# Neighbourhood attention over 416 keys in one run: latents in blocks of eight columns, biases expanded in DRAM

## The chip, the cores and the metric

The kernel runs on one core of a Trainium2 chip. The metric is the device time of one execution in microseconds (us), as the median of several executions. TensorE (PE) multiplies matrices, VectorE (DVE) and ScalarE (ACT) work on vectors, GpSimd (POOL) does vector work and starts DMAs, SyncE (SP) only starts DMAs. 16 DMA engines serve the core.

## The reference

Two layers of a diffusion transformer over 256 latents (4 rows of 64 columns) and 256 context tokens, width 1024, all in float32. Layer 0 mixes by retention, layer 1 by neighbourhood attention (32 heads of 32), each followed by an MLP of width 4096. Scales, shifts and gates come from `ada_w`, a projection of the conditioning vector. The part that the change touches:

```
rows = n // GRID_W                      # 4
kh = min(NAT_WIN_ROWS, rows)            # 4: every row is seen
kw = NAT_WIN_COLS                       # 16
row_start = jnp.clip(jnp.arange(rows) - kh // 2, 0, rows - kh)
col_start = jnp.clip(cols - kw // 2, 0, GRID_W - kw)
col_in = (cols[None, :] >= col_start[:, None]) & (cols[None, :] < col_start[:, None] + kw)
...
bias = rpb_f[:, dr_idx[None, :, None], dc_idx[:, None, :]]
bias = jnp.where(col_in[:, None, :], bias, -jnp.inf)
s_loc = jnp.einsum('bqhd,bikhd->bhqik', q_r, k_band) + bias
s_ctx = jnp.einsum('bqhd,blhd->bhql', q_r, k_c)
prob = jax.nn.softmax(jnp.concatenate([s_loc, s_ctx]), axis=-1)
```

A query sees, in each of the four rows, the 16 columns around its own, and all 256 context tokens. Its bias depends on the head, on the row difference (7 values are used) and on the column difference.

## The kernel before

**Matrix products.** Each float32 operand is split into a high and a low part (`hi`, `lo`); a product is three matmuls (`mm3`: high by high, high by low, low by high). Weights come in blocks of 512 KB: SP starts the load (`raw`, a ring of four buffers that the `ada_w` blocks, `rawa`, share), ACT casts `raw` to `hi`, DVE subtracts to get `lo` (five buffers of each).

**Order.** SP's instructions keep the order of the program (`PIN = {"sync"}`); the other engines' instructions are ordered by a scheduler, except where the text switches the order on. Every instruction is recorded at line L84, so groups are told apart by their tiles. `bg()` advances a stream in the background: one load of `ada_w` (`rawa`, SP) and its weighted sum on DVE (`acc`).

**Layer 0's MLP** runs twice over halves of the hidden width (`hf`), eight blocks (`fp`) each, then the second product. In it the bias of layer 1 is prepared in DRAM: `outside()` writes the negated table to `rpb_neg` (ACT's DMA queue) and fills `rpb_rows` with 1e30 (`far`, 14 DMAs of SP); `shifted_biases(q)`, called in `hf` 0 for `fp` 2 to 5, writes for each of the 64 query columns the 16 columns that it sees at the place of their key (79 DMAs of POOL, two for a query whose columns lie in both halves, each of 224 pieces, 32 heads by 7 row differences). `rpb_rows` is laid out by query column, head, half (32 columns), row difference, column.

**Latent order in layer 1.** `mod_aff` and `mod_split` put the latents, which come row by row, into two halves of 32 columns (`b=2`), each with its four rows, 128 latents a half. A query tile (`qt`) is a half. The keys of a head are kept in `kT` as half 0, half 1, context (512 columns).

**Attention.** 16 steps `n`: group of four heads `g = n // 2`, query tile `n % 2`. `scores(n)` forms 128 queries by 512 keys for four heads, four matmuls side by side in row groups of 32, three times (high and low parts). `soften(n)` adds the negated bias and takes the minimum in one DVE instruction per head; ACT takes the exponential with the sum. The bias tile is double: `load_bias(n + 2)` stands in `gather(n)`, in four or eight DMAs of POOL; the tile holds the bias of the 256 latent keys, and a two-part access (`bias_ap`) reads 256 zeros for the context behind them. Of the other half only the eight nearest columns can be seen; `gather` copies their 32 exponentials together (POOL), `flip` turns own half, context and these with PE transposes, and `attend` multiplies by the values. For the eight columns of the other half `rest_mm` picks the values by a selection matrix that POOL copies together (`sel`).

`q_evac` and `k_evac` split the projections into high part (ACT) and low part (DVE). Between the steps PE works on the next projections (`K`, `Q`, `V`) and on the output projection (`W`), in an order that the program writes out. PSUM has eight banks of 512 columns, given out in turn to all products, so a new product may have to wait until an earlier one is evacuated.

Of the kernel before, what the change touches and what calls it, by code (L numbers as in the profile page):

```python
# [10 lines left out]
F32 = mybir.dt.float32  # L11
F32R = mybir.dt.float32r
AF = mybir.ActivationFunctionType
# [91 lines left out]
def kernel(  # L105
# [60 lines left out]
    def tsl(t):  # L166
        return slice(t * P, (t + 1) * P)
# [225 lines left out]
    rpb_neg = dram.tile([NH, 15, 31], F32, tag="rpbn", name="rpb_neg")  # L393

    def outside():
        neg = scr("neg")
        act.dma_start(out=neg[:NH, :465], in_=rpb_in.rearrange("h r c -> h (r c)"))
        pool.tensor_scalar_mul(out=neg[:NH, :465], in0=neg[:NH, :465], scalar1=-1.0)
        act.dma_start(out=rpb_neg[:].rearrange("h r c -> h (r c)"), in_=neg[:NH, :465])
        far = scr("far")  # L400
        pool.memset(far[:], BIG)
        dst = rpb_rows[:].rearrange("q (a h) b d c -> (q a) (h b d c)", a=2)
# [3 lines left out]
    def shifted_biases(q):  # L406
        cs = min(max(q - 8, 0), GRID_W - 16)
        for b in range(2):
            c0, c1 = max(cs, HALFW * b), min(cs + 16, HALFW * (b + 1))
            if c0 < c1:  # L410
                src = rpb_neg[:, 4 : 4 + NRR, 15 - q + c0 : 15 - q + c1]
                pool.dma_start(out=rpb_rows[q][:, b, :, c0 - HALFW * b : c1 - HALFW * b], in_=src)


    pool.memset(onecol[:], 0.0)
# [178 lines left out]
    def mod_aff(pt, half, t, A, B, on_act=None, halves=False):  # L594

        tmp = scr("aff")
        for i in range(4):
            k = 4 * half + i
            a, b = A[:, k, t // 2 : t // 2 + 1], B[:, k, t // 2 : t // 2 + 1]
            o, x_ = tmp[:, tsl(i)], pt[:, tsl(i)]  # L600
            if halves:
                o = o.rearrange("p (b r c) -> p b r c", b=2, r=2)
                x_ = x_.rearrange("p (r b c) -> p b r c", b=2, r=2)
            if not (half if on_act is None else on_act):
                dve.tensor_scalar(out=o, in0=x_, scalar1=a, scalar2=b, op0=ALU.mult, op1=ALU.add)
            else:
                act.activation(out=o, in_=x_, func=AF.Identity, scale=a, bias=b)
        return tmp

    def mod_split(tmp, half, t, eng, halves=False):  # L610
        ks = slice(4 * half, 4 * half + 4)
        if halves:
            hi, lo = (
                h[:, ks, :NLAT].rearrange("p k (b r) -> p k b r", b=2)[:, :, :, 64 * t : 64 * t + 64]
                for h in (hTh, hTl)
            )
            split(tmp[:].rearrange("p (k b r) -> p k b r", k=4, b=2), hi, lo, eng)
# [661 lines left out]
    for hf in range(2):  # L1279
# [46 lines left out]
        for fp in range(len(hid), 8):  # L1326
            ht = hslot(fp)
            pb = [bank("p1") for _ in range(2)]
            us = take(2)
            mm1(us, ALL, pb)  # L1330
            pe.on = False
            dve.on = hf == 0
            evac1(pb, ALL, ht)
            if hf == 0 and fp < 6:
                residual(fp - 2, xns[fp - 2], gb, dve)
            dve.on = False
            hid.append(ht)
            if hf:
                bg(2 + fp % 2)
            elif fp > 5:  # L1340
                bg()
            if hf == 0 and fp < 6:
                for q in range(16 * (fp - 2), 16 * (fp - 1)):
                    shifted_biases(q)
        if G2 is None:
            G2 = load_gate(0, 1)
        for half in range(2):
# [142 lines left out]

    def k_evac(pb, g, a=0, b=NT):
        kT = kTs[g // 2][:, g % 2]
        act.copy(out=kT[:, 0, a:b], in_=pb[:, a:b])
        dve.tensor_sub(out=kT[:, 1, a:b], in0=pb[:, a:b], in1=kT[:, 0, a:b].bitcast(F32))

    def k_part(g, a=0, b=NT):
        k_evac(k_mm(g, a, b), g, a, b)
# [20 lines left out]

    ring = [None, None]

    def bias_at(n, j):
        i = 4 * (n % 2) + j
        return (ring[1], 0, 256) if i == 7 else (ring[0], i * 256, 7 * 256)

    def load_bias(n):

        g, qt = n // 2, n % 2
        parts = [(0, 4)] if n % 2 == 0 else [(0, 3), (3, 1)]
        for j0, nj in parts:
            tile_, o, _ = bias_at(n, j0)  # L1530
            b = tile_[:, o : o + 256 * nj]
            for r in range(4):
                pool.dma_start(
                    out=b[32 * r : 32 * r + 32].rearrange("p (h b c) -> p h b c", h=nj, b=2),
                    in_=rpb_rows[
                        HALFW * qt : HALFW * qt + HALFW, 4 * g + j0 : 4 * g + j0 + nj, :, 3 - r : 7 - r, :
                    ].rearrange("q h b d c -> q h b (d c)"),
                )

    def bias_ap(n, j):  # L1540
        tile_, o, zo = bias_at(n, j)
        base = tile_[:, o : o + 256]
        return bass.AP(base.tensor, base.offset, [list(base.ap[0]), [zo - o, 2], [1, 256]])
# [15 lines left out]

    def soften(n):  # L1560

        mn = smp.tile([P, 4], F32, tag="mn", name=nm("mn"), bufs=3)
        sm = sums[n] = smp.tile([P, 4], F32, tag="sums", name=nm("sums"), bufs=3)
        for j in range(4):
            s = Es[n, j] = scr("s")
            dve.tensor_tensor_reduce(
                out=s[:].rearrange("p (a t) -> p a t", a=2),
                in0=pss[n][j][:].rearrange("p (a t) -> p a t", a=2),
                in1=bias_ap(n, j),
                scale=1.0,  # L1570
                scalar=3.0e38,
                op0=ALU.add,
                op1=ALU.min,
                accum_out=mn[:, j : j + 1],
            )
            act.activation(
                out=s[:], in_=s[:], func=AF.Exp, scale=-1.0, bias=mn[:, j : j + 1], accum_out=sm[:, j : j + 1]
            )


    av = [None]
# [17 lines left out]

    def gather(n):  # L1600

        o = 0 if n % 2 else P
        c0 = 24 if n % 2 else 0
        for j in range(4):
            pool.tensor_copy(
                out=pt_at(n, RAW)[:, 32 * j : 32 * j + 32].rearrange("p (r c) -> p r c", r=4),
                in_=Es[n, j][:, o : o + P].rearrange("p (r c) -> p r c", r=4)[:, :, c0 : c0 + 8],
            )
        if n + 2 < NS:
            load_bias(n + 2)  # L1610

    def flip(n, sums_too=True):
        for j in range(4):
            pp = bank("ppt")
            for i, kc in enumerate((n % 2, 2, 3)):
                pe.transpose(pp[:, tsl(i)], Es[n, j][:, tsl(kc)], ident)
            w = 3 * P
            if j == 3:
# [48 lines left out]
    def rest_mm(half):  # L1667

        pr = bank("pnv")
        sels = scr("sel")  # L1670
        for qt in range(2):
            sel = sels[:, 32 * qt : 32 * qt + 32]
            pool.tensor_copy(
                out=sel.rearrange("p (r c) -> p r c", r=4),
                in_=ident.rearrange("p (r c) -> p r c", r=4)[:, :, 24 * qt : 24 * qt + 8],
            )
# [78 lines left out]
    pool.memset(ring[0][:, 7 * 256 :], 0.0)  # L1755
    pool.memset(ring[1][:, 256:1024], 0.0)
    load_bias(0)
    load_bias(1)
    for g in range(2):
        fetch(1)  # L1760
        k_part(g, NLAT, NT)
# [462 lines left out]
```

## Time and profile before

| | us |
|---|---|
| median of 3 runs | 1172.63 (1172.37 to 1175.64) |
| the profiled execution | 1173.14, its span 1171.0 |
| layer 0's MLP, `hf` 0 from `fp` 2 on (writing of the biases) | about 458 to 540 |
| `hf` 1, blocks `fp` 0 to 7, and what is prefetched for it | about 590 to 700 |
| the attention steps | about 813 to 965 |

How the rows are read: a row of the timeline or of the chain begins with the start and the length in us, then the engine, the operation, its tiles (output, arrow, inputs) and how many are drawn together (x). A group has its busy time and the mean of one in ns behind the bar, then the idle time before it and what ended that. A queue's row has packets, megabytes and the share of the time of 16 DMA engines. "PEld" is PE loading weights, beside its matmuls. `pqk` are scores, `s` the exponentials, `mn` the minima, `ppt` the transposed exponentials in PSUM and `pt` in SBUF, `pn` the projections of q and k, `pnv` of v, `pnw` the output projection, `pav` the attention's output.

### The profile page before, as it was taken

How to read it: one execution, taken by the hardware profiler on the slowest of the kernel's cores; microseconds unless marked ns; L12 is line 12 of the kernel's file. 1: busy time of each engine (PE TensorE's matmuls, PEld its weight loads, DVE VectorE, ACT ScalarE, POOL GpSimd, SP SyncE). 2: the span in 40 equal slices, each digit the busy share in tenths (PEclk: the TensorE clock that was granted, in tenths of full speed). 3: DMA queues.
4: the chain of work that ended last, by engine and by line, in shares of the span. 5: the costliest groups of instructions: out<-in, count | busy, mean ns of one | idle time of the engine just before them, and what ended most of it. 6: DMA issues, size and time to landing. Idle time of an engine off the chain costs nothing.

```text
span 1171.0 us, 17545 instructions
## 1 busy us (share of the span) xinstructions
PE 1160.9 (99%) x6687; PEld 980.6 (84%) x6687; DVE 850.3 (73%) x1363; ACT 480.8 (41%) x819; POOL 232.5 (20%) x418
## 2 busy tenths in 40 slices
PE   9999999999999999999999999999999999999997
PEld 7788888888888889888888888889888878999886
DVE  3787687777798877677866675578577589877457
ACT  3643332222323246442122333237466666756341
POOL 0102001010220241781211001223343430000001
PEclk9999999999999999999999999999999999999999
DMA  9943562544365426767666665637344335666761
GB/s 279 277 134 100 162 192 94 158 149 145 108 180 170 140 65 213 195 135 223 190 201 189 205 204 189 202 101 205 82 140 138 108 114 158 214 205 205 239 199 54
DMA packets 140115, 195.10 MB, mean 167 GB/s; under 512 B 9936, under 2 KB 81136, under 8 KB 140032
## 3 DMA queue, kind: packets, MB, share of 16 engines
q1 hardware_dynamic: 131904, 182.03, 50.6%
q0 software_dynamic: 6976, 9.39, 4.0%
q10 hardware_dynamic: 1152, 2.56, 0.7%
q8 instruction: 52, 0.85, 0.3%
q14 instruction: 31, 0.25, 0.1%
HBM read 189.12 MB, written 5.75 MB: 166 GB/s over the span
## 4 chain that ended last, share of the span: by engine, by line
PE 94%; DVE 2%; DMA 1%; ACT 1%; issue 1%; POOL 0%; ACTq 0%; DVEq 0%; SPq 0%
PE p L84 44%; PE pq L84 8%; PE pv L84 8%; PE pw L84 7%; PE pg L84 7%; PE pn L84 5%; PE pnv L84 4%; PE po L84 2%; PE ppt L84 2%; PE pnw L84 1%; PE pS L84 1%; PE pav L84 1%; PE pqk L84 1%; PE pt L84 1%; PE pada L84 1%; PE p1t L84 1%
## 5 line engine op out<-in xcount | busy, mean ns | idle before, releaser
L84 ACT CAST hi<-raw 128x1024 fp32r<-128x1024 f32 (+2 forms) x228 | 231.7, 1032 | 306.1 <-PE p L84 111.0
L84 DVE TENSOR_TENSOR lo<-raw,hi 128x1024 fp32r<-128x1024 f32 (+2 forms) x228 | 272.2, 1210 | 87.5 <-ACT hi L84 87.2
L84 PE MATMUL p<-hi,hid 128*128 128x512 f32 (+1 forms) x780 | 238.0, 386 | 0.0
L84 PEld LDWEIGHTS p<-hi,hid 128*128 128x128 f32 x780 | 145.8, 188 | 29.5
L84 PE MATMUL p<-hTl,hi 128*128 128x256 f32 (+1 forms) x512 | 165.9, 326 | 0.0
L84 PE MATMUL p<-hTh,lo 128*128 128x256 f32 (+1 forms) x512 | 165.9, 326 | 0.0
L84 PE MATMUL p<-hTh,hi 128*128 128x256 f32 (+1 forms) x512 | 162.6, 327 | 0.0
L84 PE MATMUL p<-lo,hid 128*128 128x512 f32 (+1 forms) x390 | 150.5, 386 | 0.0
L84 DVE SCALAR_TENSOR_TENSOR acc<-rawa,scol,acc 128x1024 f32<-128x1024 f32 x56 | 73.6, 1321 | 65.2 <-DMA rawa<-in_ada_w_dram 65.0
L84 PEld LDWEIGHTS p<-hTl,hi 128*128 128x128 f32 x512 | 96.5, 188 | 8.7
L84 PEld LDWEIGHTS p<-hTh,lo 128*128 128x128 f32 x512 | 96.4, 188 | 8.7
L84 PEld LDWEIGHTS p<-hTh,hi 128*128 128x128 f32 x512 | 94.2, 188 | 8.8
L84 PEld LDWEIGHTS p<-lo,hid 128*128 128x128 f32 x390 | 73.3, 188 | 14.5
L84 DVE SCALAR_TENSOR_TENSOR strips<-rawa,scol,strips 128x512 f32<-128x512 f32 x112 | 78.6, 763 | 0.0
L84 ACT CAST hid<-r 128x256 fp32r<-128x256 f32 (+1 forms) x64 | 31.9, 500 | 108.5 <-DVE r L84 108.5
L84 POOL TENSOR_TENSOR rstd<-rstd,misc 128x1 f32<-128x1 f32 x28 | 19.1, 684 | 219.6 <-DVE rstd L84 218.6
L84 ACT ACTIVATE s<-s,mn 128x512 f32<-128x512 f32 x64 | 45.5, 713 | 21.6 <-DVE mn L84 21.6
L84 PE MATMUL pw<-hi,oh 128*128 128x512 f32 x128 | 50.8, 397 | 0.0
L84 PE MATMUL pg<-hi,hTh 128*128 128x512 f32 x128 | 50.6, 395 | 0.0
L84 PE MATMUL pw<-hi,ol 128*128 128x512 f32 x128 | 50.1, 391 | 0.4 <-DVE ol L84 0.4
L84 PE MATMUL pg<-hi,hTl 128*128 128x512 f32 x128 | 49.9, 390 | 0.0
L84 PE MATMUL pw<-lo,oh 128*128 128x512 f32 x128 | 49.8, 389 | 0.0
(243 smaller groups left out, 2275.4 us busy)
## 6 DMA issues: line engine op xcount, KB each, us to landing
raw<-in_mlp_w_dram SPq DMA_DIRECT2D x128, 512.0 KB, 4.5
rawa<-in_ada_w_dram SPq DMA_DIRECT2D x80, 512.0 KB, 3.9
raw<-in_ret_w_in_dram SPq DMA_DIRECT2D x42, 512.0 KB, 4.1
raw<-in_nat_w_in_dram SPq DMA_DIRECT2D x24, 512.0 KB, 4.3
rawq<-in_ada_w_dram SPq DMA_DIRECT2D x16, 512.0 KB, 5.9
raw<-in_ret_w_o_dram SPq DMA_DIRECT2D x16, 512.0 KB, 3.7
bias<-rpb_rows POOLq DMA_DIRECT2D x32, 128.0 KB, 2.9
raw<-in_nat_w_o_dram SPq DMA_DIRECT2D x8, 512.0 KB, 4.0
```

The lines of the kernel that those rows point to most:

```text
L84: r = f(*args, **kwargs)
```

## The change

1. The latents of layer 1 lie by blocks of eight columns (`b=8` in `mod_aff`, `mod_split`): eight blocks of 4 rows by 8 columns. `q_evac` puts a query tile back into rows of 32 columns, which takes two instructions on ACT for one and four on DVE for one, per group of heads.
2. `kT` is ordered half 0, context, half 1, so that a query tile's 128 own keys, the context and the 32 nearest of the other half are 416 columns in one run (`seen(n)`): 0 to 415 or 96 to 511. `k_evac` of a whole group takes two pieces on each engine.
3. Scores, reductions, exponentials have 416 columns. `gather`'s copies are contiguous; `rest_mm` takes its selection from the identity, and the four copies to `sel` go.
4. `rpb_rows` is by query column, five blocks of eight key columns, head, row difference, column. It is filled by 20 DMAs of 224 KB (SP). `shifted_biases` writes pieces of at most eight columns, in 99 DMAs of POOL, up to three queries of the same remainder by eight in one (170 blocks of 224 pieces).
5. New: `expanded_biases(i)`, called at each `fp` of `hf` 1, five DMAs of SP each, writes `rpb_all` in DRAM: by query tile, query, head, key; a DMA has 1024 runs of 32 floats.
6. The bias tile is single (`ring[0]`). `load_bias(n + 1)` stands at the end of `soften(n)`: two DMAs of POOL, the own 128 columns and the 32 near ones of four heads.

```diff
-    rpb_rows = dram.tile([64, NH, 2, NRR, HALFW], F32, tag="rpbr", name="rpb_rows")
+    NB = 5
+    rpb_rows = dram.tile([64, NB, NH, NRR, 8], F32, tag="rpbr", name="rpb_rows")
+    rpb_all = dram.tile([2, P, NH, 32 * NB], F32, tag="rpba", name="rpb_all")
...
-        for i in range(NH * NRR * GRID_W // 1024):
-            sp.dma_start(out=dst[:, 512 * i : 512 * i + 512], in_=far[:])
+        for i in range(64 * NB * 2 // P):
+            sp.dma_start(out=dst[P * i : P * i + P, :448], in_=far[:, :448])
+            sp.dma_start(out=dst[P * i : P * i + P, 448:], in_=far[:, :448])
...
+    def bias_rows():
+        groups = [[q] for q in range(8)]
+        groups += [[q for q in range(a, b) if q % 8 == m] for a, b in ((8, HALFW), (HALFW, 49)) for m in range(8)]
+        groups += [[q] for q in range(49, 64)]
+        jobs = []
+        for g in groups:
+            cs = min(max(g[0] - 8, 0), GRID_W - 16)
+            c = cs
+            while c < cs + 16:
+                e = min(c // 8 * 8 + 8, cs + 16)
+                jobs.append((g, c, e))
+                c = e
+        return jobs
...
+    def expanded_biases(i):
+        half, r = i // 4, i % 4
+        for b in range(NB):
+            sp.dma_start(
+                out=rpb_all[half, 32 * r : 32 * r + 32, :, 32 * b : 32 * b + 32],
+                in_=rpb_rows[HALFW * half : HALFW * half + HALFW, b, :, 3 - r : 7 - r, :].rearrange(
+                    "q h d c -> q h (d c)"
+                ),
+            )
...
             if hf:
                 bg(2 + fp % 2)
+                expanded_biases(fp)
...
     def q_evac(p):
...
-            act.mul(out=q[:, 0], in_=pb[:, :NLAT], mul=QS)
-            dve.scalar_tensor_tensor(
-                out=q[:, 1], in0=pb[:, :NLAT], scalar=QS, in1=q[:, 0].bitcast(F32),
-                op0=ALU.mult, op1=ALU.subtract,
-            )
+            for b in range(2):
+                act.mul(
+                    out=q[:, 0, tsl(b)].rearrange("p (r g c) -> p r g c", g=4, r=4),
+                    in_=pb[:, tsl(b)].rearrange("p (g r c) -> p r g c", g=4, r=4),
+                    mul=QS,
+                )
+            for r in range(4):
...
+                dve.scalar_tensor_tensor(
+                    out=lo, in0=src, scalar=QS, in1=hi.bitcast(F32), op0=ALU.mult, op1=ALU.subtract
+                )
...
     def load_bias(n):
...
+        b = ring[0][:].rearrange("p (h k) -> p h k", h=4)
+        src = rpb_all[qt, :, 4 * g : 4 * g + 4, :]
+        own, near, o = (32, 0, 96) if qt else (0, P, 3 * P)
+        pool.dma_start(out=b[:, :, 3 * P * qt : 3 * P * qt + P], in_=src[:, :, own : own + P])
+        pool.dma_start(out=b[:, :, o : o + 32], in_=src[:, :, near : near + 32])
+
+    def seen(n):
+
+        return slice(96 * (n % 2), 96 * (n % 2) + NK)
...
-                    pss[n][j][:], lhsT=q[js, a, tsl(qt)], rhs=k[js, b, :], start=(i == 0), stop=(i == 2),
+                    pss[n][j][:, :NK], lhsT=q[js, a, tsl(qt)], rhs=k[js, b, seen(n)], start=(i == 0), stop=(i == 2),
...
     def soften(n):
...
+        if n + 1 < NS:
+            load_bias(n + 1)
```

SP in the middle of `hf` 1, where `raw` are the MLP's weights and `rawa` those of the background stream; before:

```order
L84 DMA rawa_5546<-in_ada_w_dram 128x2x512
L84 DMA rawa_5559<-in_ada_w_dram 128x2x512
L84 DMA raw_5567<-in_mlp_w_dram 128x4x256
L84 DMA raw_5573<-in_mlp_w_dram 128x4x256
L84 DMA rawa_5637<-in_ada_w_dram 128x2x512
L84 DMA rawa_5640<-in_ada_w_dram 128x2x512
L84 DMA rawa_5643<-in_ada_w_dram 128x2x512
L84 DMA raw_5649<-in_mlp_w_dram 128x4x256
L84 DMA raw_5655<-in_mlp_w_dram 128x4x256
```

and after:

```order
L84 DMA rawa_5573<-in_ada_w_dram 128x2x512
L84 DMA rawa_5586<-in_ada_w_dram 128x2x512
L84 DMA rpb_all<-rpb_rows 1024x1x32 x5
L84 DMA raw_5599<-in_mlp_w_dram 128x4x256
L84 DMA raw_5605<-in_mlp_w_dram 128x4x256
L84 DMA rpb_all<-rpb_rows 1024x1x32
L84 DMA rawa_5669<-in_ada_w_dram 128x2x512
L84 DMA rawa_5672<-in_ada_w_dram 128x2x512
L84 DMA rpb_all<-rpb_rows 1024x1x32 x7
L84 DMA rawa_5675<-in_ada_w_dram 128x2x512
L84 DMA raw_5686<-in_mlp_w_dram 128x4x256
L84 DMA raw_5692<-in_mlp_w_dram 128x4x256
```

The weights keep their order; the new transfers stand between them, in clumps of one to seven, 40 in all.

POOL over two attention steps, where `pt<-s` are `gather`'s copies (one per head) and the DMAs load the bias; before:

```order
L84 DMA bias_6891<-rpb_rows 32x8x128
L84 COPY pt_6978<-s_7732 128x32
L84 COPY pt_6978<-s_7735 128x32
L84 DMA bias_6891<-rpb_rows 32x8x128 x3
L84 COPY pt_6979<-s_7879 128x32
L84 DMA bias_6891<-rpb_rows 32x6x128
L84 COPY pt_6979<-s_7882 128x32
L84 COPY pt_6979<-s_7885 128x32
L84 DMA bias_6891<-rpb_rows 32x6x128
L84 COPY pt_6979<-s_7888 128x32
L84 DMA bias_6891<-rpb_rows 32x6x128 x2
L84 DMA G_6892<-rpb_rows 32x2x128 x4
```

and after:

```order
L84 COPY pt_7041<-s_7770 128x32
L84 COPY pt_7041<-s_7773 128x32
L84 DMA bias_6964<-rpb_all 128x4x128
L84 DMA bias_6964<-rpb_all 128x4x32
L84 COPY pt_7041<-s_7776 128x32
L84 COPY pt_7041<-s_7779 128x32
L84 COPY pt_7042<-s_7929 128x32
L84 COPY pt_7042<-s_7932 128x32
L84 DMA bias_6964<-rpb_all 128x4x128
L84 DMA bias_6964<-rpb_all 128x4x32
```

A step has two loads in place of four or eight; they are for the step that follows, where they were for the one after it, and two of a step's four copies stand behind them.

DVE at the second pair of q, between a step's `lo` weights and the copies of the transposes (`ppt`); before:

```order
L84 TENSOR_TENSOR lo_7741<-raw_7738,hi_7740 128x1024
L84 TENSOR_TENSOR lo_7746<-raw_7743,hi_7745 128x1024
L84 SCALAR_TENSOR_TENSOR qT_6630<-pn_7750,qT_6630 128x256
L84 SCALAR_TENSOR_TENSOR qT_6630<-pn_7751,qT_6630 128x256
L84 COPY pt_6979<-ppt_7809 128x384
```

and after:

```order
L84 TENSOR_TENSOR lo_7787<-raw_7784,hi_7786 128x1024
L84 TENSOR_TENSOR lo_7792<-raw_7789,hi_7791 128x1024
L84 SCALAR_TENSOR_TENSOR qT_6687<-pn_7796,qT_6687 128x2x32 x4
L84 SCALAR_TENSOR_TENSOR qT_6687<-pn_7797,qT_6687 128x2x32 x4
L84 COPY pt_7042<-ppt_7863 128x384
```

The place is the same, with eight instructions of 64 columns for two of 256.

More of the change, by code (lines that the diff above doesn't have):

```diff
@@ L389 @@
     HALFW = GRID_W // 2
-    rpb_rows = dram.tile([64, NH, 2, NRR, HALFW], F32, tag="rpbr", name="rpb_rows")
+    NB = 5
+    rpb_rows = dram.tile([64, NB, NH, NRR, 8], F32, tag="rpbr", name="rpb_rows")
+    rpb_all = dram.tile([2, P, NH, 32 * NB], F32, tag="rpba", name="rpb_all")
     rpb_in = nat_rpb[0]
-    rpb_neg = dram.tile([NH, 15, 31], F32, tag="rpbn", name="rpb_neg")
+    rpb_neg = dram.tile([NH, NRR, 31], F32, tag="rpbn", name="rpb_neg")
     def outside():
@@ L398, in outside @@
         pool.tensor_scalar_mul(out=neg[:NH, :465], in0=neg[:NH, :465], scalar1=-1.0)
-        act.dma_start(out=rpb_neg[:].rearrange("h r c -> h (r c)"), in_=neg[:NH, :465])
+        act.dma_start(out=rpb_neg[:].rearrange("h r c -> h (r c)"), in_=neg[:NH, 4 * 31 : 11 * 31])
         far = scr("far")
         pool.memset(far[:], BIG)
-        dst = rpb_rows[:].rearrange("q (a h) b d c -> (q a) (h b d c)", a=2)
-        for i in range(NH * NRR * GRID_W // 1024):
-            sp.dma_start(out=dst[:, 512 * i : 512 * i + 512], in_=far[:])
@@ L406, in shifted_biases @@
[L406 to L412, printed above, removed]
+        dst = rpb_rows[:].rearrange("q b (a h) d c -> (q b a) (h d c)", a=2)
+        for i in range(64 * NB * 2 // P):
+            sp.dma_start(out=dst[P * i : P * i + P, :448], in_=far[:, :448])
+            sp.dma_start(out=dst[P * i : P * i + P, 448:], in_=far[:, :448])
@@ new lines, in shifted_biases @@
+    def shifted_biases(g, c, e):
+        q = g[0]
+        b = c // 8 - (0 if q < HALFW else 3)
+        src = rpb_neg[:, :, 15 - q + c : 15 - q + e]
+        dst = rpb_rows[q][b, :, :, c % 8 : c % 8 + e - c]
+        n = e - c
+        if len(g) == 1:
+            src, dst = (t.rearrange("h d c -> (h d) c") for t in (src, dst))
+        else:
+            src, dst = (
+                bass.AP(t.tensor, t.offset, [[step, len(g)], [t.ap[1][0], NH * NRR], [1, n]])
+                for t, step in ((src, 0), (dst, (8 * NB + 1) * NH * NRR * 8))
+            )
+        pool.dma_start(out=dst, in_=src)
@@ L1342 @@
             if hf == 0 and fp < 6:
-                for q in range(16 * (fp - 2), 16 * (fp - 1)):
-                    shifted_biases(q)
+                jobs = bias_rows()
+                for job in jobs[len(jobs) * (fp - 2) // 4 : len(jobs) * (fp - 1) // 4]:
+                    shifted_biases(*job)
         if G2 is None:
@@ L1465, in q_evac @@
             q = q_of(2 * p + i)
-            act.mul(out=q[:, 0], in_=pb[:, :NLAT], mul=QS)
-            dve.scalar_tensor_tensor(
-                out=q[:, 1], in0=pb[:, :NLAT], scalar=QS, in1=q[:, 0].bitcast(F32),
-                op0=ALU.mult, op1=ALU.subtract,
-            )
+            for b in range(2):
[5 more added lines that the diff above has]
+            for r in range(4):
+                src = pb[:, :NLAT].rearrange("p (b g r c) -> p b g r c", b=2, g=4, r=4)[:, :, :, r]
+                hi, lo = (
+                    q[:, e].rearrange("p (b r g c) -> p b r g c", b=2, g=4, r=4)[:, :, r] for e in range(2)
+                )
+                dve.scalar_tensor_tensor(
+                    out=lo, in0=src, scalar=QS, in1=hi.bitcast(F32), op0=ALU.mult, op1=ALU.subtract
+                )
     def q_pair(p):
@@ L1492, in k_evac @@
         kT = kTs[g // 2][:, g % 2]
-        act.copy(out=kT[:, 0, a:b], in_=pb[:, a:b])
-        dve.tensor_sub(out=kT[:, 1, a:b], in0=pb[:, a:b], in1=kT[:, 0, a:b].bitcast(F32))
+        parts = []
+        if a == 0:
+            parts.append((
+                pb[:, :NLAT].rearrange("p (b t) -> p b t", b=2),
+                [kT[:, e].rearrange("p (b t) -> p b t", b=4)[:, 0:4:3] for e in range(2)],
+            ))
+        if b == NT:
+            parts.append((pb[:, NLAT:], [kT[:, e, P : P + NLAT] for e in range(2)]))
+        for src, (hi, lo) in parts:
+            act.copy(out=hi, in_=src)
+            dve.tensor_sub(out=lo, in0=src, in1=hi.bitcast(F32))
     def k_part(g, a=0, b=NT):
@@ L1519 @@
     ring = [None, None]
-    def bias_at(n, j):
-        i = 4 * (n % 2) + j
-        return (ring[1], 0, 256) if i == 7 else (ring[0], i * 256, 7 * 256)
+    NK = NLAT + P + 32
     def load_bias(n):
         g, qt = n // 2, n % 2
[L1528 to L1543, printed above, removed]
+        b = ring[0][:].rearrange("p (h k) -> p h k", h=4)
[5 more added lines that the diff above has]
+        return slice(96 * (n % 2), 96 * (n % 2) + NK)
     sums, rrs, Es, pts, pss = {}, {}, {}, {}, {}
@@ L1566, in soften @@
             dve.tensor_tensor_reduce(
-                out=s[:].rearrange("p (a t) -> p a t", a=2),
-                in0=pss[n][j][:].rearrange("p (a t) -> p a t", a=2),
-                in1=bias_ap(n, j),
+                out=s[:, seen(n)],
+                in0=pss[n][j][:, :NK],
+                in1=ring[0][:, 512 * j : 512 * j + 512][:, seen(n)],
                 scale=1.0,
@@ L1576, in soften @@
             act.activation(
-                out=s[:], in_=s[:], func=AF.Exp, scale=-1.0, bias=mn[:, j : j + 1], accum_out=sm[:, j : j + 1]
-            )
+                out=s[:, seen(n)], in_=s[:, seen(n)], func=AF.Exp, scale=-1.0, bias=mn[:, j : j + 1],
+                accum_out=sm[:, j : j + 1],
+            )
+        if n + 1 < NS:
+            load_bias(n + 1)
     av = [None]
@@ L1614, in flip @@
             pp = bank("ppt")
-            for i, kc in enumerate((n % 2, 2, 3)):
+            for i, kc in enumerate((3 * (n % 2), 1, 2)):
                 pe.transpose(pp[:, tsl(i)], Es[n, j][:, tsl(kc)], ident)
```

30 lines of the change are left out of this document (9 added, 21 removed).

## The prediction

> **What bounds the kernel now.** I read the head of the page first, then the chain by engine, then windows by stage.
>
> ```profile
> span 1171.0 us, 17545 instructions
> ...
> PE 1160.9 (99%) x6687; PEld 980.6 (84%) x6687; DVE 850.3 (73%) x1363; ACT 480.8 (41%) x819; POOL 232.5 (20%) x418
> ```
>
> ```profile
> PE 94%; DVE 2%; DMA 1%; ACT 1%; issue 1%; POOL 0%; ACTq 0%; DVEq 0%; SPq 0%
> ```
>
> PE (TensorE) is busy for 1160.9 of 1171.0 us, and 94% of the chain that ended last is PE's. So an edit moves the end in two ways only: by changing PE's own instructions, or by making PE wait where it does not wait now. The second question is one of slack, stage by stage:
>
> ```profile
> 476.00:540.00 64.00, 64.00 (x284) 53.01 (x283) 49.12 (x52) 25.16 (x33) 45.67 (x78) 1.00 0.73 167
> ...
> 612.00:700.00 88.00, 88.00 (x390) 72.90 (x389) 61.87 (x73) 29.47 (x42) 9.23 (x14) 1.00 0.64 198
> ...
> 813.00:965.00 152.00, 151.88 (x1259) 123.48 (x1259) 103.70 (x262) 93.77 (x227) 61.41 (x148) 1.00 0.42 121
> ```
>
> Behind each stretch stand its length, the busy time of PE, PE's weight loads, DVE, ACT and POOL, the granted clock, the DMA share and GB/s. The first holds the writing of the shifted biases, the second the second half of layer 0's MLP, the third the attention steps. PE is full in all three, at clock 1.00. In the attention DVE has 48 us to spare and ACT 58; in the MLP it is the DMA engines that are nearest to full.
>
> **Scores (512 to 416 columns), on the path.** A step's twelve score matmuls run as three rounds of four, one row group each:
>
> ```profile
> 938.53 0.97 PE L84 MATMUL pqk<-kT,qT 32*128 32x512 f32 x12
> 939.43 0.50 PE L84 MATMUL pnw<-hi,oTh 128*128 128x512 f32 x1
> ```
>
> From the first score to the next operation is 0.90 us. What a column costs I take from a dense stretch of the chain:
>
> ```profile
> 332.02 21.76 PE pq L84 x96
> ```
>
> 21.76/96 = 0.2267 us for 512 columns, 0.443 ns a column. Three rounds of 96 fewer columns are 0.128 us, times 16 steps **-2.04 us**. If all of the 0.90 us scaled with the columns it would be 0.90 x 96/512 x 16 = -2.7; if the rounds were limited by their weight loads, 0. I take -2.04, as three rounds of 0.227 are most of the 0.90.
>
> **Softmax (64 reductions on DVE, 64 exponentials on ACT).** Mostly off the path, but one place is on it, near the end of the attention. Chain rows, then PE's row of the transposes there, and an undisturbed step's:
>
> ```profile
> 957.39 0.68 DVE s L84
> 958.12 2.93 ACT s L84 x8
> ```
>
> ```profile
> 935.89 1.47 PE L84 MATMUL ppt<-cst,s 128*128 128x128 f32 x12
> 937.20 0.27 PE L84 MATMUL ppt<-cst,pt 128*128 128x128 f32 x1
> ```
>
> ```profile
> 960.48 1.86 PE L84 MATMUL ppt<-cst,s 128*128 128x128 f32 x12
> ...
> 962.18 0.27 PE L84 MATMUL ppt<-cst,pt 128*128 128x128 f32 x1
> ```
>
> Transposing a step takes 1.31 us (935.89 to 937.20), here 1.70: 0.39 us is waiting for the four exponentials. They get shorter by up to 2.93 x 96/512 = 0.55 us, so I take **-0.39 us** (bounds 0 and -0.39, as no more waits there).
>
> **The q and k evacuations, cut into pieces.** Per pair of heads DVE has eight pieces of 64 columns for two of 256, ACT four of 128 for two:
>
> ```profile
> L84 DVE SCALAR_TENSOR_TENSOR qT<-pn,qT 128x256 fp32r<-128x256 f32 x8 | 3.0, 418 | 0.0
> ```
>
> ```profile
> L84 DVE TENSOR_TENSOR kT<-pn,kT 128x512 fp32r<-128x512 f32 x6 | 4.1, 688 | 4.8 <-ACT kT L84 4.8
> ```
>
> (688 - 418)/256 = 1.05 ns a column, so a piece of 64 is about 0.22 us, and a pair 1.75 in place of 0.84: +0.9 us of DVE, four times. A k of 512 columns in two pieces of 256 costs +0.15. Room for it in the sums there is plenty; but at one place PE already waits on just this:
>
> ```profile
> 885.64 0.75 DVE L84 SCALAR_TENSOR_TENSOR qT<-pn,qT 128x256 fp32r<-128x256 f32 x2
> ```
>
> ```profile
> 885.80 1.60 PE L84 MATMUL pqk<-kT,qT 32*128 32x512 f32 x12
> ...
> 887.34 0.50 PE L84 MATMUL pnv<-hi,hTh 128*128 128x512 f32 x1
> ```
>
> The scores take 1.54 us in place of 0.90, since their last banks come free only when DVE has evacuated both q. Done 0.9 us later, they would cost +0.9; but the reductions and exponentials ahead are shorter by some 0.4 us, and the changed order gives the scores an earlier bank (the fourth now waits for ACT). Bounds -0.64 (the wait goes) and +0.9; I take **+0.3 us**.
>
> **The bias tile, single and loaded late.** Step n+1's two loads may be issued only when step n's reductions are done. Queued behind them on POOL are two small copies per step, for PE's transposes. The tightest case is the last step:
>
> ```profile
> 959.84 0.08 DVE L84 DVE_READ_ACCUMULATOR2_ANT mn<- 128x1 f32 x1
> ...
> 964.99 0.69 DVE L84 CUSTOM_DVE_ANT_1 s<-pqk,bias 128x512 f32<-128x512 f32 x1
> ```
>
> ```profile
> bias<-rpb_rows POOLq DMA_DIRECT2D x32, 128.0 KB, 2.9
> ```
>
> ```profile
> L84 POOL DMA_DIRECT2D bias<-rpb_rows x64 | 37.0, 581 | 20.3 <-DVE mn L84 17.1 <-issue 2.9
> ```
>
> 959.92 + 2 x 0.58 + 2.9 = 964.0, 1.0 us ahead of its reader; the reader comes some 0.5 us sooner after the change. The loads are twice as large, so landing may take up to twice as long: 0 to +2.4 us. I take **0**, as the nearest row leaves half a microsecond.
>
> **The expanded biases: 40 transfers, DRAM to DRAM.** Each is 1024 runs of 128 B, on SP's queue between the weights. SP issues in order, so what stands behind a clump (up to seven) waits. No transfer of 128-B runs is in the trace. The nearest below are the 78 writes of shifted biases in 476 to 524, 224 pieces of at most 64 B each, DRAM to DRAM:
>
> ```profile
> q1 hardware_dynamic: 4237, 5.92, 44.9%
> q0 software_dynamic: 2379, 0.86, 25.9%
> ```
>
> 0.259 x 48 us x 16 engines = 199 us for 17,472 pieces, 11.4 ns each. The nearest above are the first loads (0 to 46 us), at a full queue, mostly 512-B packets, 586 B on average:
>
> ```profile
> q1 hardware_dynamic: 21371, 12.53, 102.5%
> ```
>
> 1.025 x 46 x 16/21371 = 35 ns. So one transfer is 0.73 us (1024 x 11.4/16) to 2.24 us of all engines; linear in the bytes, 14.9 ns, 0.95 us. Forty are 29 to 90 us, likeliest **38**. What is free where they stand, 590 to 700 us:
>
> ```profile
> q1 hardware_dynamic: 13759, 21.58, 63.2%
> ```
>
> (1 - 0.632) x 110 = 40 us. So the likeliest price just fits, and a clump of seven (6.7 us) is covered by the lead that weights have:
>
> ```profile
> 649.01 2.96 SPq L84 DMA_DIRECT2D raw<-in_mlp_w_dram  x2
> ```
>
> ```profile
> 662.22 2.00 ACT L84 CAST hi<-raw 128x1024 fp32r<-128x1024 f32 x2
> ```
>
> With 4 us to land these are there at 653 to 656, 6 to 9 us ahead of their cast. I take **0**; without that cover see the first rival. The Trainium skill ("DMA: Bandwidth & Descriptors", Why small descriptors are slow) gives each packet some 3 cycles beside one per 32 B: by it 128 B cost 7/19 of 512 B, an estimate of 13 ns, which changes nothing.
>
> **The shifted biases, in pieces of at most 32 B.** By the loops in the code 170 blocks of 224 pieces for 79, so 38,080 for 17,696, at 11.4 ns or less: 27 us of all engines for 12.6, +14.5 us in 476 to 540, where the share goes from 0.73 to at most 0.96. Ahead of them SP fills 20 x 224 KB for 14 x 256 KB:
>
> ```profile
> 458.06 13.67 SPq L84 DMA_DIRECT2D rpb_rows<-far  x14
> ```
>
> 13.67 x 4480/3584 = 17.1, +3.4 us for the weights behind:
>
> ```profile
> 476.30 1.05 ACT L84 CAST hi<-raw 128x1024 fp32r<-128x1024 f32 x1 [3.17 <-DMA raw<-in_mlp_w_dram]
> ...
> 489.94 1.05 ACT L84 CAST hi<-raw 128x1024 fp32r<-128x1024 f32 x1 [0.21 <-PE p L84]
> ```
>
> That cast already waits for its weights, but at 489.94 ACT waits for PE to free one of five buffers, so four cast blocks lie ahead of PE: the one of 476.30 is not used before 490, and has 12 us. Cost **0**; without that cover +3.4.
>
> **Sum.** -2.04 - 0.39 + 0.3 = -2.1 us. The profiled execution took 1173.14 us, so 1171.0; it stands 0.5 above the median of 1172.63, against which the forecast is **1170.5 us**. The halves by eight columns in the modulation keep their instruction counts and columns; bounded by nothing and their strided read, I cost them at 0 (DVE and ACT idle beside them).
>
> **Rivals.**
> 1. *The expansion fills the DMA queue* (slower). For it: 63% of the queue is taken there, 38 us go into 40. Against: the small price of small pieces. It decides where 40 transfers exceed the free 40 us and some 9 us of lead, from 1.2 us each (19 ns a run). At 1.5 us PE waits 60 - 49 = 11 us (1181 to 1182), at the 2.24 of the bound 41 (1212). Where each short write costs as much again as moving it, 30 ns in place of 14.9, a transfer takes 1.9 us and PE waits 76 - 49 = 27 (1198); the 11.4 ns of still shorter writes speak against it. The Trainium skill names such a mechanism ("DMA: Bandwidth & Descriptors", Specifications): below 512 B an engine does a read-modify-write; no run here shows 128 B. Likeliest within this rival is 1180.
> 2. *The late bias becomes the wait.* Where landing takes over 3.4 us (959.92 + 1.16 + 3.4 = 964.5, the reader's new time), the last step's reductions come late, by 2.4 us at twice the landing time; other steps follow only beyond that. The gain is gone: 1171.5 to 1173.
> 3. *The smaller pieces of the shifted biases or the fill reach PE*: the 12 us of lead are used up if weights get half their pace; 3 to 8 us, 1174 to 1179.
> 4. *The change does not do what it says*: score rounds are bound by weight loads or by DVE's bank releases; 1172.6.
>
> **How the numbers follow.** Forecast 0.51, rival 1 0.20, rival 2 0.16, rival 3 0.06, rival 4 0.07. A measurement of this kernel can tell about 0.3% (3.5 us) from no change. The forecast, rivals 2 and 4 lie within it; all bounds of gain together (2.7 + 0.39 + 0.64 = 3.7) just pass it, so faster gets 0.05. Slower: rivals 1 and 3 (0.26) less 0.01 for the part of 1 that stays under 3.5 us: 0.25. Within: 0.70. The range goes from 1168.9 (all bounds of gain) to 1188 (1.65 us a transfer); above it are some 8 in 100, with the bound at 35 ns, which is a price of four times the bytes.
>
> **What would show it.** Right: the score step at 0.77 us, the transposes near the end at 1.31, a DMA share of 0.95 or more between 590 and 700 with PE still full, each expanded transfer at about 0.95 us of the engines. Wrong: PE idle with "DMA raw" behind ACT's casts or "DMA rawa" growing behind DVE in 590 to 700 (rival 1), DVE's reductions waiting for "DMA bias" (rival 2), ACT's casts waiting for weights past 480 (rival 3), score steps still 0.90 (rival 4).

## The result and the profile after

The changed kernel took 1220.83 us (median of 6 runs, 1213.61 to 1224.29), the kernel before 1173.25 in the same runs: ratio 1.0399, 95% interval 1.0366 to 1.0432, **slower by 47 us**. The profiled execution took 1220.71 us, its span 1218.9. The forecast was 1170.5 in a range of 1168.9 to 1188.0.

The head of its page: span, busy engines, PE in 40 slices with the granted clock below, and the chain by engine.

```profile
span 1218.9 us, 17588 instructions
PE 1176.0 (96%) x6687; PEld 988.3 (81%) x6687; DVE 847.5 (70%) x1393; ACT 478.1 (39%) x833; POOL 254.7 (21%) x370
PE   9999999999999999998769998999999999999997
PEclk9999999999999999998889999899999999999999
PE 35%; DVE 2%; DMA 2%; ACT 2%; SPq 1%; issue 0%; DVEq 0%; ACTq 0%
```

PE has the same 6687 matmuls. It idles 42.9 us where it idled 10.1 (1171.0 - 1160.9), and is busy 15.1 us longer: 32.8 + 15.1 = 47.9, the difference of the spans. The dip lies in slices 19 to 21, 549 to 640 us. Windows of that stretch (length, busy PE, PE's weight loads, DVE, ACT, POOL, clock, DMA share, GB/s):

```profile
476.00:540.00 64.00, 64.00 (x284) 53.01 (x283) 40.76 (x45) 22.10 (x30) 30.69 (x25) 1.00 0.94 112
540.00:557.00 17.00, 17.00 (x76) 14.08 (x76) 8.04 (x7) 2.41 (x3) 7.33 (x5) 1.00 0.94 131
557.00:606.00 49.00, 36.08 (x133) 28.23 (x133) 20.80 (x20) 5.99 (x6) 20.55 (x14) 0.86 1.02 129
606.00:640.00 34.00, 24.08 (x96) 18.89 (x95) 16.85 (x16) 4.20 (x4) 15.00 (x14) 0.85 1.09 145
640.00:700.00 60.00, 56.25 (x241) 45.91 (x240) 39.97 (x39) 18.25 (x25) 38.64 (x61) 0.97 0.91 224
```

Up to 557 us PE is full. Then 22.8 us of the idle time (12.9 + 9.9) fall between 557 and 640, where the DMA engines are over 100% "busy" (packets overlap) at 129 to 145 GB/s; before, the windows shown had 167 and 198 GB/s at shares of 0.73 and 0.64. So the engines were held by something that moves few bytes. SP issues the first expansion transfer only at 599 us. Setting the start of the same matmul of both traces side by side, PE is 5.8 us late at 564 us of before's time, 18.6 at 582, 31.6 at 606, 37.4 at 643, and 49.1 from 721 on: two thirds of it by when SP had issued 4 of the 40 transfers.

Who waits for whom in 557 to 606 (us in total, times, longest):

```profile
ACT hi L84 <- DMA raw<-in_mlp_w_dram: 42.4, 6, 10.1
DVE acc L84 <- DMA rawa<-in_ada_w_dram: 29.3, 6, 6.8
...
PE p L84 <- DVE lo L84: 12.9, 3, 5.9
```

PE itself waits for DVE's `lo`. ACT's long wait is not what holds PE: `e1_single`, an experiment below in which PE is not late, has 40.0 us of it in the same stretch, in ten shorter waits. Which wait ends last shows at PE's first stop (timeline):

```profile
556.69 1.05 ACT L84 CAST hi<-raw 128x1024 fp32r<-128x1024 f32 x1 [5.83 <-DMA raw<-in_mlp_w_dram]
...
566.96 1.29 DVE L84 SCALAR_TENSOR_TENSOR acc<-rawa,scol,acc 128x1024 f32<-128x1024 f32 x1 [4.45 <-DMA rawa<-in_ada_w_dram]
...
568.16 1.22 DVE L84 TENSOR_TENSOR lo<-raw,hi 128x1024 fp32r<-128x1024 f32 x1
...
569.43 0.79 PE L84 MATMUL p<-lo,hid 128*128 128x512 f32 x1 [5.87 <-DVE lo L84]
```

The first part of this block (`hi`) is ready at 557.7. DVE makes its `lo` 10.4 us later, since the instruction ahead of it waits for a block of the background stream (`rawa`). PE's three other long waits up to 640 us (3.98, 3.07 and 8.69 us) look the same, with `hi` ready 8 to 14 us before DVE starts `lo`.

Why these blocks are late shows in the view of DMAs in 476 to 540 (queue 0 is POOL's software queue; the last number of an issue row is the time to landing):

```profile
q0 software_dynamic: 1668, 0.53, 41.2%
...
raw<-in_mlp_w_dram SPq DMA_DIRECT2D x9, 512.0 KB, 8.7
rawa<-in_ada_w_dram SPq DMA_DIRECT2D x4, 512.0 KB, 9.8
rpb_rows<-rpb_neg POOLq DMA_DIRECT2D x8, 21.0 KB, 12.8
```

The same view of the kernel before:

```profile
q0 software_dynamic: 2528, 0.92, 19.8%
...
raw<-in_mlp_w_dram SPq DMA_DIRECT2D x12, 512.0 KB, 4.8
rawa<-in_ada_w_dram SPq DMA_DIRECT2D x7, 512.0 KB, 5.0
rpb_rows<-rpb_neg POOLq DMA_DIRECT2D x48, 14.0 KB, 3.7
```

Fewer bytes of shifted biases (0.53 for 0.92 MB) take twice the engines' time, one such DMA lands in 12.8 us in place of 3.7, and the blocks of both streams land in 8.7 and 9.8 in place of 4.8 and 5.0. POOL is slow as well: in its timeline there is a pause ahead of each of these DMAs, in which it waits for nothing that the profile shows ("issue").

```profile
537.14 1.46 POOL L84 DMA_DIRECT2D rpb_rows<-rpb_neg  x1 [1.58 <-issue]
541.27 1.47 POOL L84 DMA_DIRECT2D rpb_rows<-rpb_neg  x1 [2.66 <-issue]
```

These are DMAs that write two or three queries in one; by the loops in the code 46 of the 99 do. POOL issues the last of the 99 at 666 us, where before issued the last of its 79 at 524.

### The profile page after: what moved, and what is told of

Its sections match the earlier page's. It is cut to its first block, busy times and chain, and to the rows that moved or that the text cites. A ratio compares the mean times of both kernels' runs of the same rounds, so it can differ in the third digit from the quotient of the medians.

```text
span 1218.9 us, 17588 instructions
## 1 busy us (share of the span) xinstructions
PE 1176.0 (96%) x6687; PEld 988.3 (81%) x6687; DVE 847.5 (70%) x1393; ACT 478.1 (39%) x833; POOL 254.7 (21%) x370
## 5 line engine op out<-in xcount | busy, mean ns | idle before, releaser
L84 PE MATMUL p<-hi,hid 128*128 128x512 f32 (+1 forms) x780 | 245.9, 396 | 3.8 <-ACT hi L84 3.8
L84 PEld LDWEIGHTS p<-hi,hid 128*128 128x128 f32 x780 | 150.4, 194 | 36.2 <-ACT hi L84 5.0
L84 PE MATMUL p<-lo,hid 128*128 128x512 f32 (+1 forms) x390 | 155.7, 399 | 23.3 <-DVE lo L84 23.3
L84 POOL DMA_DIRECT2D rpb_rows<-rpb_neg x99 | 96.5, 978 | 103.5 <-issue 85.8
L84 PEld LDWEIGHTS p<-lo,hid 128*128 128x128 f32 x390 | 75.8, 194 | 41.5 <-DVE lo L84 26.1
L84 ACT CAST hid<-r 128x256 fp32r<-128x256 f32 (+1 forms) x64 | 31.6, 501 | 58.4 <-DVE r L84 58.3
```

Of the source, the lines that this page charges most:

```text
L84: r = f(*args, **kwargs)
```

## The experiments

All times are medians beside the kernel before on the same chip (1172.7 to 1173.2 us there).

### Which of the two DRAM steps it is

*Without the expansion.* The 40 DMAs go; zeros are written to `rpb_all` in layer 0, so the attention reads zeros as biases.

```diff
                 bg(2 + fp % 2)
-                expanded_biases(fp)
```

> The changed kernel without the 40 DMAs of the expansion; the tensor of expanded biases is filled with zeros by 20 DMAs of POOL in layer 0's retention, so the attention reads zeros as biases. The shifted biases are written as in the changed kernel. Theory M or S: PE is late by about 32 us from the first half of the MLP, and the attention gives back 1 to 2: 1203. Theory E: about 1172.

Measured: 1218.52 us, ratio 1.0381 (1.0360 to 1.0402). PE is 45.1 us late by the end of the MLP, where the changed kernel is 49.1. The expansion is not the cause, and neither is SP standing still behind transfers that wait for their rows, as there are none here. The 17 us lost after SP's first transfers, which had looked like their share, come for the most part from the writing of the shifted biases too, which POOL goes on with until 658 us here.

*The expansion alone*, added to the kernel before:

```diff
+    def expanded_biases(i):
+        half, r = i // 4, i % 4
+        for b in range(5):
+            sp.dma_start(
+                out=rpb_all[half, 32 * r : 32 * r + 32, :, 32 * b : 32 * b + 32],
+                in_=rpb_rows[HALFW * half : HALFW * half + HALFW, :, b % 2, 3 - r + b // 2, :],
+            )
...
                 bg(2 + fp % 2)
+                expanded_biases(fp)
```

> The kernel before, with 40 more DMAs on SP's queue at the same place of the program (DRAM to DRAM, 1024 runs of 128 B each, from its own rows of biases to a tensor that nothing reads). Nothing else changes. Theory E: most of the 47 us, 1200 or more. If the expansion costs what PE loses in the changed kernel after 640 us: about 17 us, 1190. If the expansion costs only where the weights have lost their lead already: 1173 to 1176.

Measured: 1174.01 us, ratio 1.0016 (1.0003 to 1.0028). In its profiled execution PE loses 1.1 us, at one place, between 706 and 721 us, where five transfers stand ahead of two weights. Queue 1 in 540 to 706 us, of before and of this run:

```profile
q1 hardware_dynamic: 20226, 33.06, 63.5%
```

```profile
q1 hardware_dynamic: 47035, 34.17, 71.3%
```

In 166 us 30 transfers (3.9 MB) fell into this window, and 2.8 MB of weights out of it: at 105.4 us for 33.06 MB the remaining weights are 96.4 of 118.4 us, so one transfer costs an estimated 22/30 = 0.73 us of all engines, 11.5 ns for a run of 128 B.

### What makes the shifted biases dear

*One query per DMA*: the same pieces in 170 DMAs.

```diff
-                jobs.append((g, c, e))
+                jobs += [([q], c + q - g[0], e + q - g[0]) for q in g]
```

> The changed kernel, but every DMA of the shifted biases writes one query (170 DMAs of 224 pieces in place of 99, 47 of which hold two or three queries). Same pieces, same bytes. Theory M (the DMAs that hold several queries are what is dear: about 30 ns a piece of all engines against 7 for the single ones late in the same run): PE is not late any more at the end of the first half of the MLP, the software queue's time falls from about 1000 us of engines to 300, and only what the expansion costs is left, about 17 us: 1188. Theory S (the number of small pieces is dear, however they are grouped): still about 1220. Theory E (the expansion is all of it): still about 1220.

*The same 99 DMAs with their loops exchanged*: 224 rows outside, two or three queries inside.

```diff
-                bass.AP(t.tensor, t.offset, [[step, len(g)], [t.ap[1][0], NH * NRR], [1, n]])
+                bass.AP(t.tensor, t.offset, [[t.ap[1][0], NH * NRR], [step, len(g)], [1, n]])
```

> The changed kernel, with the same 99 DMAs, but those of several queries go over the 224 rows outside and the queries inside. Same pieces, same bytes, same number of DMAs. If a DMA of several queries is dear because its outermost loop of two or three puts it on two or three of the 16 engines, this is as good as single queries: about 1188, with landings of weights back near 5 us. If it is dear because it reads one source several times, or by its three loops, it stays near 1220.

Measured: 1173.75 us, ratio 1.0008 (0.9995 to 1.0020), and 1173.46, ratio 1.0006 (0.9989 to 1.0024). Both are 47 us better than the changed kernel and not to be told from the kernel before. The second moves the same bytes, by as many DMAs, with the same source read several times: only the order of the loops differs. So neither the number of pieces (theory S) nor the longer fill, which both runs keep, is the cause. (The expectation's 47 DMAs of several queries are 46.) POOL's pauses go with the loops too; its 99 DMAs in the changed kernel and with exchanged loops, busy time and idle time ahead:

```profile
L84 POOL DMA_DIRECT2D rpb_rows<-rpb_neg x99 | 96.5, 978 | 103.5 <-issue 85.8 <-DMA rpb_rows<-rpb_neg 14.3 <-DMA rpb_neg<-neg 3.2
```

```profile
L84 POOL DMA_DIRECT2D rpb_rows<-rpb_neg x99 | 69.0, 705 | 19.5 <-DMA rpb_rows<-rpb_neg 15.5 <-DMA rpb_neg<-neg 3.3 <-issue 0.2
```

*One query per DMA, but an outermost loop of 2, or of 8* (interleaved rows):

```diff
-            src, dst = (t.rearrange("h d c -> (h d) c") for t in (src, dst))
+            src, dst = (
+                bass.AP(t.tensor, t.offset, [[t.ap[1][0], 2], [2 * t.ap[1][0], NH * NRR // 2], [1, n]])
+                for t in (src, dst)
+            )
```

> As e1_single (170 DMAs, one query each), but each goes over its 224 rows in two interleaved halves, outermost loop 2, inner loop 112. No DMA holds several queries, no source is read twice. Theory O (a DMA is spread over as many engines as its outermost loop allows, so an outermost loop of 2 or 3 is dear, whatever it holds): the software queue's time per piece is back to 25 to 35 ns of engines, weights land in 10 us and more, 1210 to 1250. Rival (several queries in one, with the source read again, were dear): as e1_single, 1174.

> As e7_outer2 with an outermost loop of 8 and an inner loop of 28. Theory O: half of the engines serve a DMA, so the price lies far nearer to the 224-row form: 1174 to 1180. Rival (any third loop is dear): like e7_outer2.

Measured: with 2, 1292.78 us, ratio 1.1016 (1.0997 to 1.1036), far worse than expected; now all 170 DMAs have the bad form and not 46 of 99. With 8, 1177.32, ratio 1.0041 (1.0026 to 1.0056). So several queries in a DMA are not needed for the loss: an outermost loop of 2 is enough. Interleaved rows alone are not enough, as the run with 8 shows. Queue 0 in 476 to 540 us (with the weights' landing for the worst), in the order one query (224 outside), loops exchanged, 2, 8:

```profile
q0 software_dynamic: 3152, 0.53, 24.9%
```

```profile
q0 software_dynamic: 2173, 0.72, 30.4%
```

```profile
q0 software_dynamic: 1941, 0.49, 46.3%
...
raw<-in_mlp_w_dram SPq DMA_DIRECT2D x9, 512.0 KB, 9.3
```

```profile
q0 software_dynamic: 3004, 0.60, 21.1%
```

The share of 64 us x 16 engines over the megabytes; the time of a piece is an estimate with the mean of 24 B (0.92 MB in 38,080; 52 B before):

| outermost loop | DMAs | us of engines per MB | ns a piece | MLP weights land in | last one issued at | ratio |
|---|---|---|---|---|---|---|
| 224 (before, pieces to 64 B) | 79 | 220 | 11.4 | 4.8 us | 524 us | 1 |
| 3, 2 or 224 (changed) | 99 | 796 | 19 | 8.7 | 666 | 1.0399 |
| 224, one query | 170 | 481 | 11.6 | 5.4 | 588 | 1.0008 |
| 224, several queries inside | 99 | 432 | 10.4 | 6.9 | 554 | 1.0006 |
| 2, one query | 170 | 968 | 23 | 9.3 | 746 | 1.1016 |
| 8, one query | 170 | 360 | 8.7 | 5.2 | 592 | 1.0041 |

With exchanged loops the weights land late too, but only until 554 us; PE loses 1.7 us there in the profiled execution. So what counts beside the landing time is how long the late landing lasts.

### What the attention gives

In `e1_single` PE gains 0.7 us over the attention (from 0.30 late to 0.38 early against before), not the 2.1 of the forecast. Two score steps after a k evacuation are late, by 0.81 and 0.95 us. Timeline at the first of them, ACT, DVE and the scores:

```profile
855.84 0.36 ACT L84 CAST kT<-pn 128x256 fp32r<-128x256 f32 x1
...
857.34 0.41 DVE L84 TENSOR_TENSOR kT<-pn,kT 128x256 fp32r<-128x256 f32 x1
...
857.79 0.37 ACT L84 CAST kT<-pn 128x256 fp32r<-128x256 f32 x1 [1.59 <-DVE kT L84]
...
858.19 0.42 DVE L84 TENSOR_TENSOR kT<-pn,kT 128x256 fp32r<-128x256 f32 x1 [0.44 <-ACT kT L84]
```

ACT's second cast waits for DVE's first subtraction, though they touch different columns. By the code the first piece is two strided blocks that enclose the second, which may be why one waits for the other; that was not tested. In a row behind each other the four take 2.8 us, and ACT stands still for 1.59 of it, with the transposes' copies behind.

*Both casts first:*

```diff
-        for src, (hi, lo) in parts:
-            act.copy(out=hi, in_=src)
-            dve.tensor_sub(out=lo, in0=src, in1=hi.bitcast(F32))
+        for src, (hi, _) in parts:
+            act.copy(out=hi, in_=src)
+        for src, (hi, lo) in parts:
+            dve.tensor_sub(out=lo, in0=src, in1=hi.bitcast(F32))
```

> As e1_single, with the two pieces of a k evacuation in another order: both casts on ACT, then both subtractions on DVE (in the changed kernel cast, subtraction, cast, subtraction, where ACT's second cast waited 1.59 us for DVE's first subtraction at 857.8 us). If that chain is what the attention lost, the two late score steps (0.81 and 0.95 us) go: 1.3 to 1.7 us faster than e1_single, 1172. Rival: the pieces' time itself is what is late: no change, 1173.7.

Measured: 1171.18 us, ratio 0.9991 (0.9981 to 1.0001), 11 runs. The same place:

```profile
856.16 0.63 ACT L84 CAST kT<-pn 128x256 fp32r<-128x256 f32 x2
...
857.65 0.74 DVE L84 TENSOR_TENSOR kT<-pn,kT 128x256 fp32r<-128x256 f32 x2
...
858.39 0.89 PE L84 MATMUL pqk<-kT,qT 32*128 32x416 f32 x12
```

The waiting between the two engines is gone, and against before PE gains 2.95 us between 810 and 985 us (from 1.05 late to 1.90 early). This is the best version found, 1.5 us below the kernel before by the medians; the interval just reaches no change.

*The expansion elsewhere*, to win back the 0.8 us that it costs there: on POOL's queue, on ACT's queue, or seven per block in place of five on SP's.

```diff
-            sp.dma_start(
+            pool.dma_start(
```

> As e9_kfix, with the 40 DMAs of the expansion on POOL's queue in place of SP's. If the 0.8 to 1.1 us that PE loses near 715 us is the weights standing behind a clump of five expansions on SP's queue, it goes: 1171.2. If the engines' time for them is what counts, or POOL takes long to issue 1024 runs (over 2 us each) and its own work comes late, no better than e9_kfix or worse: 1172 to 1176.

> As e9_kfix, with the expansions on ACT's DMA queue in place of SP's. If standing behind them on one queue is what delays the weights, the 0.8 us goes: 1170.4. If ACT's own casts now stand behind the issues (about 0.5 to 1.9 us each), or the engines' time counts, 1171.2 or more.

> As e9_kfix, with seven expansions per block of the second half of the MLP in place of five, so that they are through two blocks earlier and no clump of five stands ahead of the first weights of the second product (in e9_kfix SP took 4.66 us for the clump at 704.42 and ACT then waited 10.91 us for weights). If that last clump is the 0.8 us, it goes: 1170.4. If any clump of this size costs, it only comes elsewhere: 1171.2 or more.

Measured: POOL 1184.50 us, ratio 1.0100 (1.0084 to 1.0115); ACT 1191.68, ratio 1.0157 (1.0139 to 1.0175); seven per block 1173.27, ratio 0.9996 (0.9981 to 1.0012). None is better. On SP's queue the transfers are spread from 520 to 709 us, up to 650 mostly one at a time. POOL can send them only behind its last shifted biases, from 585 us on, and in clumps of up to eleven:

```profile
599.81 4.76 POOL L84 DMA_DIRECT2D rpb_all<-rpb_rows  x6
```

This is 0.79 us each, so that POOL would take over 2 us for each was wrong. Why its version loses is not shown: of the weights issued in 600 to 700 us the MLP's land in 4.6 us and the background stream's in 5.2, beside 4.7 and 5.6 in `e9_kfix`. PE's first long wait (3.7 us, at 640) comes where DVE waits for `rawa` again and ACT stands still behind DVE for 18.69 us, 10.86 in `e9_kfix`. On ACT evacuations stand behind the transfers, the first of which wait for `rpb_rows`: in the group of its `r`, 14.7 us of the idle time ahead ended with those DMAs.

```profile
L84 ACT ACTIVATE r<-p 128x256 f32<-128x256 f32 (+1 forms) x64 | 30.0, 471 | 31.7 <-DMA rpb_rows<-rpb_neg 14.7 <-PE p L84 9.8 <-POOL neg L84 4.8
```

## Why the prediction was wrong

**The step that failed: "The shifted biases, in pieces of at most 32 B", taken as 0.** It multiplied pieces by 11.4 ns, and the price of a piece was right where the loops are as before (11.6 and 10.4 ns). What it left out is the form of the 46 merged DMAs. In the changed kernel, with two or three queries outermost, a piece costs an estimated 19 ns, such a DMA lands in 12.8 us, and the blocks of weights beside it in 8.7 and 9.8; POOL is at it until 666 us and not 540. At 563.4 us PE stood still for the first time, and 49.1 us were lost by 721. The cover was also looked for in the wrong stream: the 12 us of lead were counted at ACT's casts of the MLP's weights, and what ended PE's long waits was DVE, held by the background stream's blocks. One sign came true and said nothing: the engines' share in 476 to 540 is 0.94, forecast at most 0.96, but at 112 GB/s for 167. Item 4 of the change's list names the form, "up to three queries in one"; I treated a merged DMA as three DMAs that cost one issue.

The Trainium skill has the rule ("DMA: Bandwidth & Descriptors", Why a DMA increments its semaphore by 16 and not by 1): the number of engines that serve a DMA is the largest, up to 16, that divides the outermost loops of both sides. By it an outermost 224 gives 16 engines, 8 gives 8, 3 and 2 give 3 and 2. The ratios order the same way (1.0008, 1.0041, 1.0399 for the mixture, 1.1016). The page names an exception for some copies on the software queue, which these DMAs use, and these traces have no view by engine: the number of engines itself is not shown.

**Rival 3** was the right place (weights late from the writing of the biases), but was priced at 3 to 8 us with 6 in 100: it had the weights at half their pace for a short while only. They landed in about twice the time for much longer: in 8.7 us where issued in 476 to 540, and in 8.1 where issued in 540 to 660.

**The expansion**, to which rival 1 gave 20 in 100 and 1180 us, was taken at 0 and costs 1.1 (`e4_before_expand`). A transfer takes 0.73 us of the engines for the 0.95 estimated. The cover held except at the last clump, in part by luck: the transfers do not all stand in 590 to 700 us, as the prediction had it. In `e4_before_expand` SP issues the first at 501 and 14 of the 40 before 590.

**Scores, -2.04.** Right: from the chain of the changed kernel,

```profile
869.02 0.77 PE pqk L84 x12
```

This is 0.77 us a step, 0.13 less than 0.90, 2.1 in all; in `e9_kfix` 14 of the 16 steps take 0.77 or 0.78.

**Softmax near the end, -0.39.** In `e9_kfix` 1.41 us for 1.70, so -0.29. In the changed kernel it is 1.54, and in `e1_single` 2.01, worse than before: PE waits for two of POOL's copies that stand behind the bias loads, and these take 0.75 us to issue, not 0.58.

```profile
959.83 0.75 POOL L84 DMA_DIRECT2D bias<-rpb_all  x1 [0.27 <-issue]
...
960.91 0.75 POOL L84 DMA_DIRECT2D bias<-rpb_all  x1 [0.34 <-issue]
...
961.65 0.48 POOL L84 COPY pt<-s 128x32 f32<-128x32 f32 x2
...
962.19 0.14 PEld L84 LDWEIGHTS ppt<-cst,pt 128*128 128x128 f32 x1 [0.72 <-POOL pt L84]
```

The prediction had named the copies and costed them at nothing.

**The q and k pieces, +0.3.** The size was wrong on both sides. In `e1_single` the q place got 0.70 better (its scores take 0.83 us for 1.53) and a second step 0.42, but two k places got 1.76 worse. The order of the two engines accounts for most of that: in `e9_kfix` the first is no longer late, but the second still is by 0.43 us, which stays open.

**The late bias, 0.** Right in its main part: the reductions wait for their bias once, for 2.09 us early in the attention of the changed kernel, and PE is not late there.

**Clock.** That waiting makes PE slower too was in no term; see the last section.

## What to carry to other kernels

A DMA that gathers several small ones pays only if its outermost loop stays long: put the long loop outside, on both sides, and compare its landing time and that of the transfers beside it, not the bytes. Where transfers come late, follow the full engine's own wait back to the one that ended last: the longest wait in a table, here ACT's, need not be on the path. Where an evacuation is cut into pieces that two engines take in turn, issue all pieces of the first engine before those of the second. Where a change saves 2 us on the full engine, price the form of each transfer that it adds before its bytes: here one loop order cost 47 us.

## What the runs showed of the hardware that was not expected

PE pays for a long wait a second time. After a wait of 4 us the matmuls of the changed kernel soon run at about half their pace, for 3.4 us from 587.49 on (timeline of PE):

```profile
582.08 0.61 PE L84 MATMUL p<-hi,hid 128*128 128x512 f32 x2
586.68 0.50 PE L84 MATMUL p<-lo,hid 128*128 128x512 f32 x1 [3.98 <-DVE lo L84]
...
587.49 0.60 PE L84 MATMUL p<-lo,hid 128*128 128x512 f32 x1
...
589.17 1.05 PE L84 MATMUL p<-hi,hid 128*128 128x512 f32 x2
590.03 0.63 PE L84 MATMUL p<-lo,hid 128*128 128x512 f32 x1
...
591.14 0.39 PE L84 MATMUL p<-lo,hid 128*128 128x512 f32 x1
```

From 589.17 to 590.03 two take 0.86 us, 0.43 each in place of 0.227. The granted clock of 557 to 606 is 0.86, and of the 47.9 us 15.1 are busy time that is longer, not idle time. The Trainium skill describes it ("TensorE: Matmul & The Clock Gate", Part 1: The HAM clock gate): the array runs at half clock until it has been busy for some 3.4 us. The trace agrees, with 3.4 us here and 4.4 after the wait of 5.87 us, though the first matmuls after 586.68 still go at full pace.

What stays open: why a piece costs 19 to 23 ns with a short outermost loop and 9 to 12 with a long one. Serving it by fewer engines would explain the late landing, not by itself the time per piece.
